# One encoder layer with 32 experts: rows split once into two-byte halves, expert 0's rows picked by one-hot matmuls, tables spread over expert 0's products

## The chip, the cores and the metric

The kernel runs on one core of one Trainium2 chip. The metric is the time of one execution on the device in microseconds (us), the median of three runs. The engines are called PE (TensorE), DVE (VectorE), ACT (ScalarE), POOL (GpSimd) and SP (SyncE, which here only issues transfers); PEld is PE's loading of stationary operands.

## The reference

One layer over 1024 tokens of width 1024, all in float32. What matters for the change is the end of the first half and the whole second half:

```python
h = layer_norm(ALPHA * h + mixed @ w_out, ln1_g, ln1_b)
logits = h @ w_router + b_router            # 32 experts
top_vals, top_idx = lax.top_k(logits, 4)
gates = softmax(top_vals)
# each expert e, for the tokens that chose it:
y = ((up + 1) * gate * sigmoid(1.702 * gate)) @ w_mlp2[e] + b_mlp2[e]
# gate = min(a, 7), up = clip(b, -7, 7), [a | b] = x @ w_mlp1[e] + b_mlp1[e]
h = layer_norm(ALPHA * h + sum over the 4 experts of gates * y, ln2_g, ln2_b)
```

Attention with a window, a multi-scale pool and two gated branches come before; the change leaves them as they are.

## The kernel before

Every float32 operand of a product is split into a two-byte high part (float16) and a two-byte low part (bfloat16), and each product is three matmuls: high by high, high by low, low by high. The instructions of each engine stand in the order in which the Python emits them (`manual_schedule`), so an engine that waits holds up all that is emitted for it later.

**The loop over the eight token tiles** (L587 to L617) ends the first half. For tile t it loads the old row, multiplies the mixed branches by `w_out` in two halves of 512 columns (`mth`, `mtl` hold the left operand as 8 slices by 1024 tokens), adds and normalises into the row `z`, and runs the router of earlier tiles in between: `hooks.transposed(t-1)` (eight float32 PE transposes of `z`, then `tr_out` splits them from PSUM: high half by ACT at L683, low half by DVE at L684), `logits(t-1)`, `topk(t-1)`, `pos_mm`, `place` and `gates(t-2)`, `tables(t-3)`. `hooks.step(t-1)` stands at the head of an iteration: ACT rounds one megabyte of expert 0's weights (L945) and DVE forms its low half (L950). `gates` (L742) takes the exponential of the four best logits on ACT, scales four one-hot rows by them and adds them up on DVE. `write` (L665) stores `z` twice, as `hD` (the rows that experts gather) and as `accD` (the sums).

**Behind the loop** `experts.main` (L978) takes the experts one after another, in an order `TURN` by their number of tokens; each has a fixed capacity (176 for the first, 109 to 188 for the others). An expert is six steps: four quarter products of the first matrix (L1090 to L1092), two halves of the second. The steps of neighbouring experts are interleaved in `seq`; expert 0's first four steps are steps 0 to 3, the next expert begins with step 4. Around step i the program emits: evacuation of step i-1, `post_v`, `post_a`, `post_p` (the gated activation), the split of the weights of step i+2 (`w_hi` on ACT, `w_lo` on DVE), then the matmuls. Four tables (`start`, `mid`, `end`, `x_evac`) hang further work on steps.

For an expert's rows: `onehot` builds a one-hot matrix of tokens by slots on DVE, `slot_mm` multiplies it with small columns (token number, gate) on PE, `gather` fetches the float32 rows by an indirect transfer that POOL issues (L1021), `x_tr` transposes them on PE in float32 (L1055), `x_hi` and `x_lo` split them (ACT L1066, DVE L1071).

Ahead of step 0 stand, for expert 0: slots, gather, transposes and split of its rows, and the first part of `ranks` (L773), which sorts the experts by their number of tokens, fetches expert numbers for the transfers and turns the biases. In the middle of step 0 `tables` runs the rest of `ranks`: gates' columns for all experts (L825 to L838), then the table of tokens beyond the capacities (L842 to L878); with expert 0's gates and the next expert's one-hots between. At the end of step 0 `first_rows` gathers the next expert's rows, which are transposed at the end of step 1.

Weights arrive in transfers of one megabyte that SP issues into nine buffers (`refill`); a buffer is free when DVE has formed its low half.

## Time and profile before

| | us |
|---|---|
| median of three runs (1866.14 to 1868.57) | 1866.81 |
| the profiled execution's own time | 1861.56 |
| its span, first to last instruction | 1859.7 |
| PE busy in the span | 1757.3 |
| DVE busy | 1528.2 |
| ACT busy | 1226.1 |
| POOL busy | 560.5 |

The span is one execution recorded by the hardware profiler. A line such as "L950 DVE ... wl<-raw,wh 128x2048" is line 950 of the kernel on VectorE, writing `wl` from `raw` and `wh`. Busy matmuls overlap one another, so a PE that is busy all the time is one that waits for nothing; what one matmul costs is read from the distance of two starts.

### The profile page before, as it was taken

The numbers are of one execution on the slowest core, as the hardware profiler recorded it, in microseconds if no ns is written. First come the engines' busy times: TensorE is split into PE (matmuls) and PEld (weight loads), VectorE is DVE, ScalarE is ACT, GpSimd is POOL, SyncE is SP. The second block draws the span as 40 slices with busy tenths as digits, with TensorE's granted clock in tenths as the row PEclk, the third lists the DMA queues.
The fourth block names the chain that finished last, engine by engine and source line by source line (L and its number), as shares of the span: only waits on it lengthen the run. The fifth ranks groups of instructions, "written<-read, shape, count | busy, mean of one in ns | idle before, by whom it ended". The sixth has DMA issues, their size and how long they took to land.

```text
span 1859.7 us, 53706 instructions
## 1 busy us (share of the span) xinstructions
PE 1757.3 (94%) x23150; PEld 1495.0 (80%) x23150; DVE 1528.2 (82%) x2184; ACT 1226.1 (66%) x1679; POOL 560.5 (30%) x586
## 2 busy tenths in 40 slices
PE   7998999999896899999999999999999999999990
PEld 6455554444444899999999999999999999999990
DVE  4587853234696989999989999999999999999985
ACT  4455532223121578888788788888888888888873
POOL 1336420000012532244323253233432542343211
PEclk9999999999997999999999999999999999999995
DMA  5100031112655699999999999999999999999975
GB/s 181 52 24 24 24 100 56 57 46 91 218 193 197 193 332 365 364 363 358 321 354 357 362 360 370 356 373 366 367 368 376 373 370 366 375 371 366 369 274 200
DMA packets 245955, 494.20 MB, mean 266 GB/s; under 512 B 10982, under 2 KB 32870, under 8 KB 245712
## 3 DMA queue, kind: packets, MB, share of 16 engines
q1 hardware_dynamic: 234432, 453.03, 67.5%
q0 software_dynamic: 10992, 36.62, 8.0%
q8 instruction: 184, 3.01, 0.7%
q10 hardware_dynamic: 288, 1.05, 0.1%
q14 instruction: 59, 0.48, 0.1%
HBM read 458.34 MB, written 32.33 MB: 264 GB/s over the span
## 4 chain that ended last, share of the span: by engine, by line
PE 80%; DVE 11%; ACT 3%; DMA 3%; issue 2%; POOL 0%; SPq 0%; POOLq 0%; DVEq 0%; ACTq 0%
PE mm L1090 19%; PE mm L1091 19%; PE mm L1092 19%; PE mm L110 4%; PE mm L109 4%; PE mm L111 4%; PE tr L1157 2%; PE tr L1055 2%; PE pb L109 2%; PE pb L111 2%; PE pb L110 2%; DMA raw<-in_w_mlp_dram 1%; DVE wl L950 1%; PE sl L1005 1%; DVE s L346 1%
## 5 line engine op out<-in xcount | busy, mean ns | idle before, releaser
L950 DVE SCALAR_TENSOR_TENSOR wl<-raw,wh 128x2048 bf16<-128x2048 f32 x384 | 874.5, 2286 | 46.4 <-ACT wh L945 46.1
L1090 PE MATMUL mm<-xh,wh 128*128 128x123 f16 (+30 forms) x4096 | 744.0, 223 | 0.6 <-ACT xh L1066 0.6
L1091 PE MATMUL mm<-xl,wh 128*128 128x123 bf16 (+30 forms) x4096 | 743.6, 223 | 0.3 <-DVE nv L747 0.3
L1092 PE MATMUL mm<-xh,wl 128*128 128x123 f16 (+30 forms) x4096 | 743.7, 223 | 0.0
L945 ACT ACTIVATE wh<-raw 128x2048 f16<-128x2048 f32 x384 | 725.5, 1909 | 12.6 <-PE mm L1091 8.8
L1091 PEld LDWEIGHTS <-wh 128*128 128x128 f16 x6144 | 598.2, 97 | 1.8 <-issue 1.0
L1092 PEld LDWEIGHTS <-wl 128*128 128x128 bf16 x6144 | 597.5, 97 | 2.5 <-issue 2.5
L1090 PEld LDWEIGHTS <-wh 128*128 128x128 f16 x6144 | 595.9, 97 | 0.9
L1091 PE MATMUL mm<-al,wh 128*128 128x123 bf16 (+30 forms) x2048 | 370.7, 222 | 1.9 <-DVE al L1148 1.9
L1090 PE MATMUL mm<-ah,wh 128*128 128x123 f16 (+30 forms) x2048 | 371.0, 223 | 0.3 <-ACT ah L1137 0.3
L1092 PE MATMUL mm<-ah,wl 128*128 128x123 f16 (+30 forms) x2048 | 370.8, 222 | 0.0
L1021 POOL DMA_INDIRECT x<-hD,ig x51 | 73.8, 1447 | 553.2 <-DVE st L1010 310.9
L1169 POOL DMA_INDIRECT accD<-y,is x51 | 120.3, 2359 | 225.6 <-ACT yT L1114 68.9
L109 PE MATMUL mm<-xth,wh 128*128 128x512 f16 x400 | 151.9, 380 | 1.2 <-DVE ypl L104 1.1
L110 PE MATMUL mm<-xtl,wh 128*128 128x512 bf16 x400 | 151.8, 380 | 0.0
L111 PE MATMUL mm<-xth,wl 128*128 128x512 f16 x400 | 151.7, 379 | 0.0
L1165 ACT ACTIVATE y<-tr,gt 128x512 f32<-128x512 f32 (+11 forms) x102 | 65.4, 679 | 91.7 <-PE tr L1157 48.7
L111 PEld LDWEIGHTS <-wl 128*128 128x128 bf16 x528 | 51.7, 98 | 62.5 <-issue 0.3
L110 PEld LDWEIGHTS <-wh 128*128 128x128 f16 x528 | 51.7, 98 | 56.8 <-issue 1.5
L109 PEld LDWEIGHTS <-wh 128*128 128x128 f16 x528 | 51.8, 98 | 55.2 <-issue 0.3
L163 DVE SCALAR_TENSOR_TENSOR wl<-raw,wh 128x768 bf16<-128x768 f32 (+1 forms) x30 | 24.3, 865 | 81.9 <-ACT wh L159 81.7
L1106 ACT ACTIVATE pre<-mm,b1r 128x176 f32<-128x176 f32 (+30 forms) x256 | 77.8, 370 | 12.7 <-PE mm L1092 12.5
(304 smaller groups left out, 2475.3 us busy)
## 6 DMA issues: line engine op xcount, KB each, us to landing
raw<-in_w_mlp_dram SPq DMA_DIRECT2D x384, 1024.0 KB, 11.9
raw<-in_w_in_dram SPq DMA_DIRECT2D x13, 1024.0 KB, 5.3
xt<-in_x_dram SPq DMA_DIRECT2D x16, 512.0 KB, 6.7
raw<-in_w_out_dram SPq DMA_DIRECT2D x4, 1024.0 KB, 5.1
a<-accD SPq DMA_DIRECT2D x8, 512.0 KB, 7.2
hD<-z SPq DMA_DIRECT2D x7, 512.0 KB, 2.7
accD<-z SPq DMA_DIRECT2D x7, 512.0 KB, 4.0
out_dram<-o SPq DMA_DIRECT2D x7, 512.0 KB, 2.7
```

The lines of the kernel that those rows point to most:

```text
L109: nc.tensor.matmul(ps, wh(k), xh(k), start=first and i == 0, stop=False)
L110: nc.tensor.matmul(ps, wh(k), xl(k), start=False, stop=False)
L111: nc.tensor.matmul(ps, wl(k), xh(k), start=False, stop=last and i == n - 1)
L945: nc.scalar.activation(WT[i][0][:, a:b], RAW[i, h], AF.Copy, scale=WS)
L950: nc.vector.scalar_tensor_tensor(lo[:, a:b], RAW[i, h], WS, hi[:, a:b], op0=OP.mult, op1=OP.subtract)
L1021: nc.gpsimd.indirect_dma_start(out=x[:n], out_offset=None, in_=hD, in_offset=IO(ap=ig[:n, c], axis=0))
L1090: nc.tensor.matmul(ps[:, j], wh[:, k, fs], h[:, k, :Cr], start=k == 0, stop=False)
L1091: nc.tensor.matmul(ps[:, j], wh[:, k, fs], l[:, k, :Cr], start=False, stop=False)
L1092: nc.tensor.matmul(ps[:, j], wl[:, k, fs], h[:, k, :Cr], start=False, stop=k == KT - 1)
L1106: nc.scalar.activation(o[:, j], ps[:, j], AF.Identity, scale=0.5 / WS, bias=b1r[:, f0 + g + j, r:r + 1])
L1165: nc.scalar.activation(E[r]["ys"][j][:n, c * 512:(c + 1) * 512], E[r]["yp"][j][:n].rearrange("p a b -> p (a b)"), AF.Copy, scale=E[r]["gt" ...
L1169: nc.gpsimd.indirect_dma_start(out=accD, out_offset=IO(ap=E[r]["is_"][:n, j:j + 1], axis=0), in_=E[r]["ys"][j][:n], in_offset=None, comput ...
```

## The change

- `mth` and `mtl` are laid out by token tile, and a tile's part of them is used again, once its products are done, for the row's high and low half: `row` writes the high half (ACT) and the low half (DVE) straight from `z`, for all 1024 columns at once, and the last normalisation steps also take 1024 columns at once, except for tile 7.
- `transposed` makes sixteen two-byte transposes of the halves and two copies, both on ACT. `hD` holds the two halves, 4096 bytes a row as before, stored by two transfers on SP's queue.
- `gates`: a second exponential on ACT over all 32 logits, one DVE instruction in place of three.
- Expert 0's rows are not gathered: 128 matmuls of the halves by its one-hots (`x0_mm`), most of them placed around tile 7's router, and eight evacuations (`x0_out`).
- The other experts' gathered halves are transposed in two-byte form and copied: one ACT and one DVE copy of up to 1024 columns.
- `ranks` yields once more; its parts stand in the middle and at the end of step 0, in the middle of step 1 and at the end of step 2. The next expert's rows are gathered in the middle of step 2 and transposed in the middle of step 3.
- The last steps take the activation ahead of the split of weights.

```diff
@@ loop over the token tiles
+        if t == NT - 1:
+            hooks.x0_mm(range(3), range(6))
+            hooks.pos_mm(t - 1)
+            hooks.x0_mm(range(3, 4), range(6))
+        if t < NT - 1:
+            ln.apply(z, g1, b1, z, slice(0, D))
+            hooks.row(t, 0, KT)
+        else:
+            for h in range(2):
+                ln.apply(z, g1, b1, z, slice(h * 512, (h + 1) * 512))
+                hooks.row(t, h * 4, h * 4 + 4)
+                hooks.x0_mm(range(4 + h, 5 + h), range(6))
         hooks.write(t, z)
     hooks.place(NT - 2)
-    for h in range(2):
-        hooks.tr_out(NT - 1, h)
+    hooks.transposed(NT - 1)
     hooks.logits(NT - 1)
     hooks.topk(NT - 1)
+    hooks.x0_mm(range(4), range(6, KT))
     hooks.pos_mm(NT - 1)
     hooks.place(NT - 1)
+    hooks.gates(NT - 2)
+    hooks.x0_mm(range(4, 7), range(6, KT))
+    hooks.x0_mm(range(6, 7), range(6))
+    hooks.x0_mm(range(7, 8), range(KT))
+    hooks.x0_out()
@@ Router
+    def row(self, t, a, b):
+        nc, (hi, lo) = self.nc, self.rows
+        z = self.z[t][:, a * P:b * P].rearrange("p (k q) -> p k q", q=P)
+        nc.scalar.activation(hi[:, t, a:b], z, AF.Copy)
+        nc.vector.tensor_sub(lo[:, t, a:b], z, hi[:, t, a:b])
+    def x0_mm(self, tiles, ks):
...
+            for k in (2 * k2, 2 * k2 + 1):
+                for t in tiles:
+                    for j in range(2):
+                        nc.tensor.matmul(self.px[k2][:, k % 2], self.rows[j][:, t, k], self.moe.oh0(t),
...
     def transposed(self, t):
-        for h in range(2):
-            self.tr_mm(t, h)
-            self.tr_out(t, h)
+        nc, tk = self.nc, slice(t * P, (t + 1) * P)
+        self.hT[t] = []
+        for j, (dt, ident) in enumerate(((F16, "ident16"), (BF16, "identb"))):
+            tp = self.pt.tile([P, KT, P], dt, name="tp")
+            for k in range(KT):
+                nc.tensor.transpose(tp[:, k], self.rows[j][:, t, k], self.C[ident])
+            o = self.hb.tile([P, KT, P], dt, name="hh" if j == 0 else "hl")
+            nc.scalar.activation(o, tp, AF.Copy)
+            self.hT[t].append(o)
+            row = self.rows[j][:, t]
+            nc.sync.dma_start(self.hD[tk, j * D:(j + 1) * D], (row.bitcast(F16) if j else row).rearrange("p k q -> p (k q)"))
@@ gates
         nc.scalar.activation(e4, vm[:, :4], AF.Exp, bias=nv, accum_out=den)
+        nc.scalar.activation(lg, lg, AF.Exp, bias=nv)
         nc.vector.reciprocal(den, den)
-        nc.vector.tensor_scalar(e4, e4, den, None, op0=OP.mult)
-        nc.vector.tensor_mul(eq, eq, e4[:, :, None].to_broadcast([P, 4, NE]))
-        nc.vector.tensor_reduce(G, eq.rearrange("p k e -> p e k"), axis=AX.X, op=OP.add)
+        nc.vector.scalar_tensor_tensor(G, lg, den, mask, op0=OP.mult, op1=OP.mult)
@@ experts: rows of one expert
         def xparts(r):
+            return [(i, s0, n, lo) for i, (s0, n) in enumerate(E[r]["tiles"]) for lo in range(2)]
         def x_tr(r, part):
+            i, s0, n, lo = part
+            dt, ident = ((F16, C["ident16"]), (BF16, C["identb"]))[lo]
+            tp = pt.tile([P, KT, n + n % 2], dt, name="tr")[:, :, :n]
+            for k in range(KT):
...
+        def x_out(r, part):
...
+            if lo:
+                nc.vector.tensor_copy(E[r]["xl"][:, :, s0:s0 + n], tp)
+            else:
+                nc.scalar.activation(E[r]["xh"][:, :, s0:s0 + n], tp, AF.Copy)
@@ experts: what hangs on the first steps
-        slot_mm(0, 0, 2)
-        gather(0)
...
-        at(mid, 0, tables)
-        at(end, 0, first_rows)
+        def order():
+            next(rk)
+            refill()
+            evac(0, *groups(0)[0])
+        def late():
+            next(rk)
+            LATE["y"] = [[LATE["a"].tile([P, D], F32, name=f"y{b}{j}") for j in range(2)] for b in range(2)]
+            for y in LATE["y"][0] + LATE["y"][1]:
+                nc.gpsimd.memset(y, 0.0)
+        def slots0():
+            slot_mm(0)
+            targets(0)
+            onehot(1)
+        at(mid, 0, next, rk)
+        at(end, 0, order)
+        at(mid, 1, next, rk)
+        at(end, 2, late)
+        at(end, 1, slots0)
+        at(mid, 2, slot_mm, 1)
+        at(mid, 2, gather, 1)
         for r in range(1, NR):
...
             for j, part in enumerate(parts):
...
+                if r == 1:
+                    at(mid, 3, x_tr, r, part)
+                    at(end, 3, x_out, r, part)
@@ experts: around a step
+            product = 0 < i <= NS and seq[i - 1][0] == 1
+            if product and i >= NS - 3:
+                post_a(i - 1)
+                post_p(i - 1)
+                product = False
             if split:
                 w_hi(n, 0)
```

## Rows read from the trace of the kernel before

**Rows 1.** The page: the chain that ended last, by engine.
```profile
PE 80%; DVE 11%; ACT 3%; DMA 3%; issue 2%; POOL 0%; SPq 0%; POOLq 0%; DVEq 0%; ACTq 0%
```

**Rows 2.** Busy time by stretch: us, PE, PEld, DVE, ACT, POOL, PE clock, DMA, GB/s.
```profile
480.00:570.00 90.00, 79.75 (x513) 40.08 (x513) 82.58 (x198) 18.43 (x33) 14.16 (x50) 0.98 0.50 176
572.65:573.26 0.61, 0.61 (x25) 0.59 (x24) 0.40 (x1) 0.00 (x0) 0.49 (x2) 1.00 0.04 13
600.00:615.00 15.00, 12.32 (x148) 11.72 (x147) 10.37 (x60) 2.63 (x4) 2.84 (x13) 0.85 0.07 22
615.00:640.00 25.00, 21.82 (x292) 21.37 (x290) 22.65 (x36) 14.48 (x17) 13.26 (x17) 1.00 0.72 220
1400.00:1500.00 100.00, 100.00 (x1646) 99.60 (x1644) 96.08 (x105) 85.53 (x102) 40.20 (x29) 1.00 1.05 371
```

**Rows 3.** DVE's timeline, one iteration of the token loop: start us, us, instruction.
```profile
540.36 2.29 DVE L950 SCALAR_TENSOR_TENSOR wl<-raw,wh 128x2048 bf16<-128x2048 f32 x1
...
544.41 0.14 DVE L747 TENSOR_SCALAR nv<-vm 128x1 f32<-128x1 f32 x1
...
546.08 1.28 DVE L684 TENSOR_TENSOR hl<-tp,hh 128x512 bf16<-128x512 f32 x2
547.28 0.68 DVE L604 SCALAR_TENSOR_TENSOR z<-pb,xt 128x512 f32<-128x512 f32 x1
...
549.04 0.18 DVE L708 SCALAR_TENSOR_TENSOR lg<-mm,br 128x32 f32<-128x32 f32 x1
...
551.11 0.74 DVE L76 SCALAR_TENSOR_TENSOR z<-z,ln_mv,g 128x512 f32<-128x512 f32 x1
...
554.01 2.29 DVE L950 SCALAR_TENSOR_TENSOR wl<-raw,wh 128x2048 bf16<-128x2048 f32 x1
```

**Rows 4.** ACT's timeline in the same iteration.
```profile
544.58 0.30 ACT L750 ACTIVATE e<-vm,nv 128x4 f32<-128x4 f32 x1 [8.21 <-DVE nv L747]
...
544.88 1.06 ACT L683 ACTIVATE hh<-tp 128x512 f16<-128x512 f32 x2
...
548.11 1.90 ACT L945 ACTIVATE wh<-raw 128x2048 f16<-128x2048 f32 x1
```

**Rows 5.** Timelines of DVE and ACT elsewhere: instructions of the new sizes.
```profile
1835.28 2.48 DVE L1508 SCALAR_TENSOR_TENSOR a<-a,sums,g 128x1024 f32<-128x1024 f32 x2
...
1828.52 1.06 ACT L1485 ACTIVATE j<-a 128x1024 f32<-128x1024 f32 x1 [11.76 <-DVE ln_st L59]
```

**Rows 6.** From tile 7 to step 4: a piece of the chain, then PE's timeline.
```profile
572.87 0.70 DVE z L604
...
595.96 0.31 PE L1090 MATMUL mm<-xh,wh 128*128 128x176 f16 x1 [0.58 <-ACT xh L1066]
...
639.95 0.22 PE L1090 MATMUL mm<-xh,wh 128*128 128x138 f16 x1
```

**Rows 7.** Busy time by stretch as in Rows 2, PE's clock behind the token loop.
```profile
576.00:578.00 2.00, 0.20 (x2) 0.10 (x1) 1.90 (x6) 0.00 (x0) 0.00 (x0) 0.77 1.05 406
...
598.00:600.00 2.00, 2.00 (x16) 2.00 (x14) 1.29 (x6) 0.39 (x2) 1.35 (x6) 0.50 1.04 384
```

**Rows 8.** Chain of waits: float32 transposes, of a short and of a full tile.
```profile
631.58 0.59 PE tr L1055 x8
...
665.99 0.44 PE tr L1055 x4
```

**Rows 9.** PE's timeline near the end: the wait before the last product.
```profile
1804.12 0.21 PE L1091 MATMUL mm<-al,wh 128*128 128x109 bf16 x1 [1.85 <-DVE al L1148]
```

**Rows 10.** The same DVE instruction beside POOL's memsets and without them.
```profile
625.73 2.64 DVE L1123 TENSOR_SCALAR pre<-pre 128x704 f32<-128x704 f32 x1
...
641.48 0.52 DVE L1123 TENSOR_SCALAR pre<-pre 128x704 f32<-128x704 f32 x1
```

**Rows 11.** Weights, issue to landing, for 640 to 840 us and 1640 to 1760 us.
```profile
DMA to landing us min/median/max: 5.5/8.1/10.3
...
DMA to landing us min/median/max: 13.8/15.6/19.4
```

More of the change, by code (lines that the diff above doesn't have):

```diff
@@ L665, in write @@
     def write(self, t, z):
-        nc = self.nc
-        q = nc.scalar if t == NT - 1 else nc.sync
-        q.dma_start(self.hD[t * P:(t + 1) * P, :], z)
+        q = self.nc.scalar if t == NT - 1 else self.nc.sync
         q.dma_start(self.accD[t * P:(t + 1) * P, :], z)
-    def tr_mm(self, t, h):
-        nc = self.nc
-        self.tp[t, h] = tp = self.pt.tile([P, 4, P], F32, name="tp")
-        for k in range(4):
-            nc.tensor.transpose(tp[:, k], self.z[t][:, (h * 4 + k) * P:(h * 4 + k + 1) * P], self.C["identf"])
@@ new lines, in x0_mm @@
+    def x0_mm(self, tiles, ks):
+        nc, c = self.nc, self.moe.c0
+        for k2 in range(ks[0] // 2, (ks[-1] + 2) // 2):
+            if k2 not in self.px:
+                ps = self.pb.tile([P, 512], F32, name="pb") if k2 < 3 else self.pt.tile([P, 4, P], F32, name="tp")
+                self.px[k2] = (ps if k2 < 3 else ps.rearrange("p a b -> p (a b)"))[:, :2 * c].rearrange("p (k c) -> p k c", c=c)
+            for k in (2 * k2, 2 * k2 + 1):
+                for t in tiles:
+                    for j in range(2):
+                        nc.tensor.matmul(self.px[k2][:, k % 2], self.rows[j][:, t, k], self.moe.oh0(t),
+                                         start=t == 0 and j == 0 and k % 2 == 0, stop=t == NT - 1 and j == 1 and k % 2 == 1,
+                                         skip_group_check=True)
@@ L1019, in gather, with targets @@
                 nc.vector.tensor_copy(ig[q, c], E[r]["pl"][q, i, 0:1])
-                x = wk1.tile([P, D], F32, name=f"x{i}")
+                x = wk1.tile([P, 2 * D], F16, name=f"x{i}")
                 nc.gpsimd.indirect_dma_start(out=x[:n], out_offset=None, in_=hD, in_offset=IO(ap=ig[:n, c], axis=0))
                 xs.append(x)
-            rows(r, 0, 5 if r else 2)
+            E[r].update(xs=xs, xh=None)
+            targets(r)
+        def targets(r):
+            E[r]["st"] = st = sm.tile([P, 2, 8], F32, name="st")
+            E[r]["is_"] = is_ = sm.tile([P, 2], I32, name="is")
+            for i, (s0, n) in enumerate(E[r]["rows"]):
+                nc.vector.tensor_copy(st[:n, i, :5], E[r]["pl"][:n, i, :5])
             for i, (s0, n) in enumerate(E[r]["rows"]):
@@ L1215, in main @@
             if r > 1:
[L1216 to L1218 removed]
+                at(start, max(b - 9, 3), onehot, r)
+                at(end, max(b - 8, 3), slot_mm, r)
+                at(start, max(b - 7, 4), gather, r)
             parts = xparts(r)
             for j, part in enumerate(parts):
[L1221 to L1224 removed]
+                if r == 1:
+                    at(mid, 3, x_tr, r, part)
+                    at(end, 3, x_out, r, part)
+                else:
+                    s_ = b - 1 - len(parts) + j
+                    at(end, s_, x_tr, r, part)
+                    at(x_evac, s_ + 1, x_out, r, part)
         def run(table, i):
@@ L1248, in main @@
                 w_hi(n, 1)
-            if 0 < i <= NS and seq[i - 1][0] == 1:
+            if product:
                 post_p(i - 1)
@@ L1257, in main @@
                         run(mid, i)
-                    if j < len(gs) - 1:
+                    if i and j < len(gs) - 1:
                         evac(i, g, nf)
```

161 lines of the change are left out of this document (66 added, 95 removed).

## The prediction

> **What bounds the kernel now.** I first read the page's chain by engine: PE carries four fifths of it [rows 1]. Busy time by stretch says where that holds and where it does not [rows 2]. Inside the experts (1400 to 1500 us) PE is busy 100.00 of 100.00 us, with DVE at 96.08 close behind and DMA moving 371 GB/s; an instruction of another engine is worth nothing there, a PE instruction is worth its own length. In the token loop (480 to 570) it is the other way round: DVE is busy 82.58 of 90 us and PE 79.75. Between loop and experts (600 to 640) neither is full. So the change is priced in three places: the loop by DVE's order, the passage by its chain, the rest by PE.
>
> In DVE's timeline of one iteration [rows 3] one instruction follows another; from one weight split at 540.36 to the next at 554.01 an iteration takes 13.65 us. ACT is mostly idle there and runs ahead: its rounding of the next weights starts at 548.11, six us before DVE asks for them [rows 4].
>
> **The loop.** I lay the new order on the same iteration, counting from the weight split as 0, for tiles 2 to 5.
> - The gates start at 4.05 (544.41) and last 1.67 us, up to 546.08. One DVE instruction replaces three, but it waits for a second exponential on ACT, which I take at the 0.30 us of the first [rows 4]: 1.05 us in all, so 0.6 less.
> - The two subtractions from PSUM go: 546.08 to 547.28, 1.20 us less. The second half of `z` is then added at 5.1 and the logits are wanted 1.76 us later (547.28 to 549.04), at 6.86.
> - They come later than that. ACT, held by the exponentials until 4.8, now makes two copies of 1024 columns, 1.06 us each by the row of that width [rows 5], up to 6.9; then come the 24 small matmuls of the logits (25 PE instructions in 0.61 us at 572.65, the logits' [rows 2]). DVE waits 0.7 us, for 7.5.
> - Top-4 and the refinement of the root take 2.07 us (549.04 to 551.11): 9.6. Normalising took four instructions, 2.90 us (551.11 to 554.01); two of 1024 columns take 2.40 by the row with two such [rows 5]: 12.0, 0.5 less.
> - Now the low half, on DVE, needs the high half from ACT: 1.06 us in which DVE has nothing else in its order; the subtraction itself takes about 1.2 (half of the 2.48 that the two of 1024 columns take in rows 5). ACT's rounding of the next weights now stands behind the high half instead of ahead of it: 12.0 + 1.06 + 1.90 and the hand-overs give 15.1 for the next split.
>
> That is 15.1 against 13.65, 1.4 us more for each of four tiles. Tile 0 has no gates, no old subtraction and no wait: 3.05 more at its end, 0.5 less in normalising, 2.55. Tile 1 loses 1.2 of that again, 1.35. Tile 6 has no weights behind it, 0.7. Tile 7's first half is shorter by 1.8. In sum tile 7's second half starts 8.5 us later than at 572.87. PE needs about 12 us an iteration and gives no help. Ends: 5 if ACT's hand-overs cost less than I put, 10.4 if tile 7 gives nothing back. POOL's copies keep their place; on SP two 256 KB stores take the place of one, with no one waiting.
>
> **From tile 7 to step 4.** Before, this takes 67.1 us: 572.87 to 639.95 [rows 6], of which expert 0's matmuls start at 23.1. In the new order, from the start of tile 7's second half: its sums, the root and tile 6's top-4 up to 3.9 (3.83 in rows 3); normalising, high and low half for 512 columns at a time up to 9.3; transposes and two ACT copies up to 11.3, logits 12.0 (1.9 us later than before); top-4 and place 14.2. PE has 40 of the 128 one-hot matmuls left at 13.5, when tile 7's positions are issued. Between 615 and 640 us 292 matmuls, nearly all of 176 columns, took 21.82 us [rows 2], 0.0747 each; 40 take 3.0, up to 16.5. So expert 0 starts at about 16.7 instead of 23.1: gather, float32 transposes and their split are gone.
>
> From there PE has at most 12.32 + 21.82 = 34.1 us of work up to step 4 [rows 2], and could be there at 51; DVE cannot. Between 600 and 640 us DVE was busy 10.37 + 22.65 = 33.0 us [rows 2]: six weight splits, columns, overflow table, one-hots, activations. All of it stays ahead of step 4's rows, now behind step 0 (96 matmuls, 7.2 us) and the ranks' first matmuls and biases (3.2 us, an estimate: 40 matmuls more and a hand-over): 16.7 + 7.2 + 3.2 + 33.0 = 60.1, and 61 with the last copy of the next expert's rows. The stall for their gather falls under this, so it costs nothing unless DVE gets shorter; then the gather is late next.
>
> The clock adds to that. Behind the loop PE's granted clock fell from 1.00 to 0.50 (1.2 of 2.4 GHz) while it had next to nothing to do, at 576 to 578, and was still 0.50 at 598 to 600, in matmuls; from 615 on it was 1.00 [rows 2, 7]. The one-hot matmuls fill the first part of the hole and leave about 6 us of it. Ends: 0 if the clock holds, 5 if it stays low through step 0; I take 2.5. Sum 63.5: 3.6 us less than before. Ends: 7 less, and 0.
>
> **The experts.** A full tile's eight float32 transposes take 0.88 us (four in 0.44), a short tile's 0.59 [rows 8]. Sixteen two-byte ones: of 128 columns, at 0.0747 × 128 / 176 = 0.054 us, take 0.87 (an estimate); for a short tile, at the 0.61 / 24 = 0.0254 us of the small logits matmuls [rows 2], 0.41. So the full tiles stay the same and eighteen experts with a short second tile save 0.18 each: 3.3 us on a PE that is full. Ends: 0 and 4. ACT's copies keep their length, DVE's get shorter by 0.2 to 0.8 us an expert, both beside PE, worth nothing while PE is full.
>
> **The end.** The last product's low half now stands ahead of a weight split on DVE, and PE's wait of 1.85 us for it goes [rows 9]. But ACT's rounding is then behind the activation, so the last split ends some 2 us later and PE waits about 1 us for that. I take 0.8 less. Ends: 2 and 0.
>
> **Sum:** +8.5 - 3.6 - 3.3 - 0.8 = +0.8 us on the profiled execution's own 1861.56, so 1862.4. That execution lies 5.25 us below the median of 1866.81; on the median I forecast 1867.6, no difference within 0.2% (3.7 us), about what a measurement of this kernel can tell from no change. The loop's loss and the passage's gain both lie on the path, and nearly cancel with the experts' gain.
>
> **Rivals.**
> 1. *Slower: the passage gains nothing.* The place is steps 0 to 3. If the clock stays at 0.50 until step 0 has ended, 5 instead of 2.5, and DVE is held up by POOL, the passage takes 68: +8.5 + 0.9 - 4.1 = +5.3, 1872. It decides from 66.5 us of passage on. For it: `late` puts POOL's four memsets at the end of step 2, ahead of the next one-hots on DVE, and one DVE instruction took 2.64 us beside those memsets where it took 0.52 without them [rows 10]. Against it: in 40 us DVE lost only that much. The Trainium skill (SBUF — State Buffer, Who interferes with whom) has DVE's two-port modes and GpSimd lock one another out for a whole instruction; the trace agrees with 2.64 against 0.52 us. By that rule alone the forecast would rise by up to 2.1 us.
> 2. *Faster: the loop loses nothing.* If ACT's high half and the rounding behind it cost DVE no wait (the hand-overs are fewer, or PE and not DVE sets the iteration), +8.5 becomes 0 to +1 and the sum is -7, 1860. For it: DVE's own work gets shorter by about a us per tile. Against it: DVE's order, in which the low half stands directly behind the high half.
> 3. *The experts give nothing back.* Weights took 8.1 us to land early and 15.6 late [rows 11], so the transfers fall behind while PE is full. If the transfers have become the bound by the end, PE's 3.3 us are lost in a wait for weights: +4.1, 1871.
>
> **How the numbers follow.** Forecast 0.36, rival 1 0.23, rival 2 0.31, rival 3 0.10. Faster by over 0.2% is rival 2: 0.31. Within: 0.36. Slower: rivals 1 and 3, 0.33. The forecast's own range is 1864 to 1871. The range for 8 in 10 takes in rivals 2 and 1 with their own unknowns (the loop at 5 and the passage 7 less: 1858.9; the loop at 10.4 and the passage at 0: 1873.1, with 2.1 from POOL 1875.2): 1859 to 1875.
>
> **What would show it.** Right: weight splits 15 us apart in the loop, a DVE wait for ACT's high half of 1 us in each; tile 7's second half at about 581; expert 0's first matmul about 17 us behind it; DVE full from there to step 4, with PE waiting 4 us or so for the last copy; PE's clock at 0.50 for some us around the start of step 0; short tiles' sixteen transposes in 0.4 us. Wrong: iterations of 13.7 us or less, PE idle within the experts, or ACT waiting for weights at the end.

## The result and the profile after

The changed kernel takes 1879.25 us (median of 5 runs, 1875.78 to 1880.85) where the kernel before takes 1866.14 (1863.22 to 1868.57): the ratio is 1.0069, with a 95% interval of 1.0053 to 1.0084. The forecast was 1867.6, no difference, with a range of 1859 to 1875. The profiled execution of the changed kernel is the median one, with a span of 1877.5 us; that of before, with a span of 1859.7, was a quick one, so the two traces differ by 17.8 us and the medians by 13.1. A second profile of each kernel (below) lies 16.4 apart.

The traces are compared in four stretches: up to tile 7's second half of `z` (the loop), from there to step 4 (the passage), from step 4 to the end of PE's last transposes (the experts), and the rest (the end). In us, with all other kernels of this study, which the experiments below explain:

| kernel | loop | passage | experts | end | span | ratio to before (95%) |
|---|---|---|---|---|---|---|
| before | 572.87 | 67.08 | 1176.08 | 43.67 | 1859.7 | |
| changed | 583.40 | 69.91 | 1177.59 | 46.60 | 1877.5 | 1.0069 (1.0053 to 1.0084) |
| forecast, against before | +8.5 | -3.6 | -4.1 | 0 | +0.8 | |
| before, second profile | 572.25 | 65.96 | 1176.64 | 43.55 | 1858.4 | |
| changed, second profile | 584.96 | 67.63 | 1177.29 | 44.92 | 1874.8 | 1.0076 (1.0062 to 1.0090) |
| loop in another order | 575.69 | 69.60 | 1177.38 | 45.73 | 1868.4 | 1.0034 (1.0021 to 1.0047) |
| fourth transpose later | 584.54 | 62.34 | 1181.31 | 45.61 | 1873.8 | 1.0073 (1.0060 to 1.0086) |
| leftover table later | 583.78 | 61.01 | 1179.82 | 45.29 | 1869.9 | 1.0062 (1.0048 to 1.0076) |
| tables earlier | 585.03 | 67.81 | 1177.38 | 46.08 | 1876.3 | 1.0071 (1.0056 to 1.0086) |
| y transposes behind | 585.04 | 67.82 | 1178.40 | 45.84 | 1877.1 | one execution |
| before with two parts | 569.57 | 68.30 | 1179.34 | 43.09 | 1860.3 | 0.9983 (0.9972 to 0.9993) |
| four edits | 575.41 | 59.24 | 1181.23 | 45.92 | 1861.8 | 0.9993 (0.9984 to 1.0003) |
| table in pieces | 575.46 | 59.07 | 1177.63 | 45.64 | 1857.8 | 0.9978 (0.9968 to 0.9988) |
| ... and 16 memsets | 574.50 | 58.87 | 1177.50 | 46.53 | 1857.4 | 0.9977 (0.9966 to 0.9989) |
| ... and 30 matmuls | 572.44 | 58.55 | 1177.87 | 45.34 | 1854.2 | 0.9972 (0.9960 to 0.9985) |

So the changed kernel lost 10.5 us in the loop, 2.8 in the passage, 1.5 in the experts and 2.9 at the end. All four (the forecast's -0.8 for the last product lies in the experts' stretch) came out worse than forecast, by 2.0, 6.4, 5.6 and 2.9. The second pair of profiles has the same signs and other sizes: 12.7, 1.7, 0.7 and 1.4.

**The loop.** DVE's timeline of one iteration of the changed kernel, which answers to [rows 3]; the bracket is the idle time before the instruction and who ended it:

```profile
549.51 2.29 DVE L978 SCALAR_TENSOR_TENSOR wl<-raw,wh 128x2048 bf16<-128x2048 f32 x1 [0.57 <-ACT wh L973]
...
562.77 1.22 DVE L687 TENSOR_TENSOR mtl<-z,mth 128x1024 bf16<-128x1024 f32 x1 [1.12 <-ACT mth L686]
564.58 2.29 DVE L978 SCALAR_TENSOR_TENSOR wl<-raw,wh 128x2048 bf16<-128x2048 f32 x1 [0.58 <-ACT wh L973]
```

An iteration takes 15.07 us (549.51 to 564.58) instead of 13.65. DVE now stands still twice at its end, 1.12 us for the row's high half and 0.58 for the next weights' rounding, which ACT used to have ready six us ahead. ACT's timeline of the same iteration, which answers to [rows 4], shows the two in one chain behind DVE's own normalising:

```profile
561.68 1.06 ACT L686 ACTIVATE mth<-z 128x1024 f16<-128x1024 f32 x1 [4.38 <-DVE z L77]
562.65 1.90 ACT L973 ACTIVATE wh<-raw 128x2048 f16<-128x2048 f32 x1
```

**The passage.** Expert 0's first matmul starts 20.45 us behind tile 7's second half (583.40 to 603.85) instead of 23.09. But step 4 starts at 653.31, 69.91 behind it, later than before. PE's timeline from the transposes of expert 1's rows to step 4:

```profile
636.53 0.62 PE L1099 MATMUL tr<-ident,x 128*128 128x128 f16 x8 [1.89 <-DMA x<-hD,ig]
...
639.32 0.37 PE L1099 MATMUL tr<-ident,x 10*128 10x10 f16 x8 [1.72 <-DMA x<-hD,ig]
646.34 0.35 PE L1099 MATMUL tr<-identb,x 10*128 10x10 bf16 x8 [6.64 <-ACT xh L1110]
...
653.31 0.23 PE L1129 MATMUL mm<-xh,wh 128*128 128x138 f16 x1
```

Four groups of transposes stand ahead of step 3's second half, each in a PSUM tile of its own, and the pool has three such tiles (`e_pt`, L1034). The fourth waits 6.64 us for ACT to copy the first one out, and everything behind it on PE waits too. Busy time by stretch (columns as in [rows 2]) shows who is full meanwhile:

```profile
604.00:614.00 10.00, 9.79 (x174) 9.50 (x172) 3.29 (x16) 2.40 (x4) 1.71 (x7) 1.00 0.01 3
614.00:634.00 20.00, 19.65 (x277) 19.44 (x278) 19.21 (x44) 10.81 (x13) 8.33 (x12) 1.00 0.94 342
634.00:640.00 6.00, 2.09 (x33) 1.64 (x31) 5.67 (x20) 0.00 (x0) 5.19 (x14) 0.85 0.78 257
640.00:646.00 6.00, 0.00 (x0) 0.00 (x0) 5.79 (x19) 3.81 (x5) 0.00 (x0) 0.50 0.11 19
646.00:652.00 6.00, 5.66 (x47) 5.64 (x46) 3.39 (x6) 0.42 (x2) 0.95 (x1) 0.52 0.87 271
```

From 614 to 646 DVE is busy 30.67 of 32 us, while PE is busy 2.09 us of the 6 up to 640, in which its granted clock falls, and not at all from 640 to 646; the matmuls behind that run at 0.50 (1.2 of 2.4 GHz). ACT is late because an instruction ahead of its copy waits for DVE, and DVE was in the table of leftover tokens, 633.57 to 641.64. ACT's timeline:

```profile
642.19 0.79 ACT L1171 ACTIVATE th<-pre 128x704 f32<-128x704 f32 x1 [9.31 <-DVE pre L1148]
...
645.27 1.15 ACT L1110 ACTIVATE xh<-tr 128x1024 f16<-128x1024 f16 x2
```

**The experts.** Between 1420 and 1520 us PE is busy for the whole time, as before. What its transposes take is read from start to start. First the kernel before, y transposes, x transposes and the matmuls behind them, and then one short tile; then the changed kernel, the same kinds, and at its end y transposes ahead of a tile of 110 rows:

```profile
664.95 1.04 PE L1157 MATMUL tr<-identf,yT 128*128 128x128 f32 x8
665.83 0.60 PE L1055 MATMUL tr<-identf,x 128*128 128x128 f32 x4
666.26 0.22 PE L1090 MATMUL mm<-xh,wh 128*128 128x138 f16 x1
...
672.12 0.66 PE L1055 MATMUL tr<-identf,x 8*128 8x8 f32 x8
672.71 0.45 PE L1005 MATMUL sl<-cols,oh 128*128 128x5 f16 x9
```

```profile
672.57 0.61 PE L1099 MATMUL tr<-identb,x 128*128 128x128 bf16 x8
673.01 0.22 PE L1129 MATMUL mm<-xh,wh 128*128 128x138 f16 x1
...
678.77 1.04 PE L1196 MATMUL tr<-identf,yT 128*128 128x128 f32 x8
679.75 0.35 PE L1099 MATMUL tr<-ident,x 8*128 8x8 f16 x8
680.03 0.23 PE L1129 MATMUL mm<-xh,wh 128*128 128x138 f16 x1
...
911.80 1.03 PE L1196 MATMUL tr<-identf,yT 128*128 128x128 f32 x8
912.67 0.55 PE L1099 MATMUL tr<-ident,x 110*128 110x110 f16 x8
```

A short tile took 0.59 us in float32 (672.12 to 672.71) and takes 2 x 0.28 in two halves (679.75 to 680.03): next to nothing is saved. A full tile took 2 x 0.43 and takes 2 x 0.44. And the y transposes, which the change does not touch, take 0.97 or 0.98 instead of 0.88 wherever the two-byte transposes of a short tile (2 to 60 rows) follow them directly, 17 times of 17. Where those of a tile of 109 to 128 rows follow, they take what they took before, 13 times of 13 (0.87 from 911.80 to 912.67). PE's weight loads show what a short group is made of; before, then after:

```profile
672.11 0.57 PEld L1055 LDWEIGHTS tr<-identf,x 8*128 8x128 f32 x8
```

```profile
679.74 0.26 PEld L1099 LDWEIGHTS <-x 8*128 8x128 f16 x8 [0.20 <-issue]
```

A single two-byte load has a row of 0.10 us, so eight in 0.26 start 0.16 / 7 = 0.023 us apart, and eight transposes 0.023 apart are 0.18 of the 0.28. The other 0.10 I read as an edge, the price of going from the short group to the next kind of work. In float32, with 0.14 for a single load, it is 0.43 / 7 = 0.061 apart, 0.49 of the 0.59, and one edge of 0.10. Two short halves have two edges. The 0.10 that the y transposes gain is a third, on the near side of the short group; a full tile's 0.44 is 8 x 0.055 and shows none. In the kernel before no short tile stands directly behind y transposes, so whether a short float32 group would cost the same there is not shown. Over all of step 4 to the last product, x and y transposes together take 79.9 us before and 81.8 after: x 35.7 and 35.95, y 44.2 and 45.9.

**The end.** PE's wait of 1.85 us [rows 9], and one of 0.32 ahead of it, are gone; three short ones of 0.56, 0.44 and 0.37 stand in their place, and up to PE's last transposes the end is 0.6 us shorter. Behind them ACT's last copy and POOL's last scatter, before and then after:

```profile
1816.07 0.69 ACT L1165 ACTIVATE y<-tr,gt 109x512 f32<-109x512 f32 x1 [0.45 <-PE tr L1157]
...
1817.52 1.52 POOL L1169 DMA_INDIRECT accD<-y,is  x1 [5.98 <-ACTq L1287]
```

```profile
1830.94 0.69 ACT L1204 ACTIVATE y<-tr,gt 109x512 f32<-109x512 f32 x1 [0.45 <-PE tr L1196]
...
1833.56 1.53 POOL L1208 DMA_INDIRECT accD<-y,is  x1 [7.89 <-issue]
```

From the end of the copy to the scatter it is 0.76 us before and 1.93 after. Within the latter wait the DMA view shows two packets of the instruction queues (`q8`, `q14`), within the former none. From the scatter to the end of the span it took 1.7 us longer in this execution.

### The profile page after: what moved, and what is told of

Same layout as the page of the kernel before. It is cut to its first block, busy times and chain, and to the rows that moved or that the text cites. A ratio compares the mean times of both kernels' runs of the same rounds, so it can differ in the third digit from the quotient of the medians.

```text
span 1877.5 us, 54612 instructions
## 1 busy us (share of the span) xinstructions
PE 1764.8 (94%) x23644; PEld 1501.0 (80%) x23702; DVE 1506.1 (80%) x2114; ACT 1240.5 (66%) x1666; POOL 510.8 (27%) x584
## 3 DMA queue, kind: packets, MB, share of 16 engines
q8 instruction: 188, 3.08, 0.7%
## 5 line engine op out<-in xcount | busy, mean ns | idle before, releaser
L1208 POOL DMA_INDIRECT accD<-y,is x51 | 92.0, 1804 | 246.7 <-DMA accD<-y,is 80.5
L110 PE MATMUL mm<-xtl,wh 128*128 128x512 bf16 x363 | 137.6, 379 | 0.0
```

The costliest lines, as they stand in the source:

```text
L110: nc.tensor.matmul(ps, wh(k), xl(k), start=False, stop=False)
L1208: nc.gpsimd.indirect_dma_start(out=accD, out_offset=IO(ap=E[r]["is_"][:n, j:j + 1], axis=0), in_=E[r]["ys"][j][:n], in_offset=None, comput ...
```

## The experiments

**Both kernels once more.** What was expected of the kernel before:

> The kernel before once more, unchanged, for a second profile: which stretch differs between two executions of one kernel. If the 2.9 us by which the changed kernel's end (from PE's last transpose to the end of the span) is longer than before's 43.7 us is the change's, this run shows 43.7 again; if it is the spread of executions, it shows 44 to 47. Time 1862 to 1869.

And of the changed one:

> The changed kernel once more, unchanged: a second profile of it and its times beside the kernels of this call. If the stalls that the first profile shows are the kernel's and not one execution's, this one has the 6.6 us wait of PE for ACT's copy in step 3 again, 69 to 70 us from tile 7's second half to step 4, and an end of 45 to 47 us behind PE's last transposes; 0.6 to 0.8% slower than before.

Before gave 1860.21 us, below the 1862 to 1869 expected, and an end of 43.55; changed gave 1877.62, an end of 44.92, and PE's wait for ACT's copy again, 5.5 us this time because the gather's two tiles came 1.6 and 1.2 us later (their transposes start at 638.13 and 640.55). Its passage took 67.63 us where 69 to 70 were expected. The end of 43.1 to 43.7 in three profiles of before and its variant, and of 44.9 to 46.6 in all eleven of the changed kernel and its variants, is therefore the change's. The constant part of it is the 1.17 us ahead of the scatter: 0.76 in each of the three, 1.92 or 1.93 in each of the eleven. From the scatter to the end of the span it is 41.6 to 42.2 us against 42.2 to 43.9, two ranges that touch.

**The loop's order.** ACT's rounding of the next weights ahead of the row's high half, DVE's weight split ahead of the row's low half:

```diff
-        hooks.step(t - 1)
...
+        self.moe.prefetch_hi(w)
         nc.scalar.activation(hi[:, t, a:b], z, AF.Copy)
+        self.moe.prefetch_lo(w)
         nc.vector.tensor_sub(lo[:, t, a:b], z, hi[:, t, a:b])
```

> Token loop only: the rounding of the next weights stands ahead of the row's high half on ACT, and the weights' low half ahead of the row's low half on DVE, so that both roundings run beside work of DVE. Theory (the loop's loss is the two waits of DVE for ACT, 1.12 and 0.57 us in each iteration of 15.06): iterations of about 13.4 us, tile 7's second half at about 573 to 575 instead of 583.4, and some 9 to 10 us less at the end than the changed kernel's 1879, 1869 to 1870. Rival (the loop is longer because PE or SP's stores set the iteration): iterations stay above 14.5 us, less than 3 us gained, 1876 or more.

1869.1 us, 8.5 less than the changed kernel's 1877.62 (by the ratios 6.5 to 7.8, with intervals that do not meet), and tile 7's second half at 575.69. DVE's timeline shows both waits gone and an iteration of 13.18 us:

```profile
516.19 2.28 DVE L979 SCALAR_TENSOR_TENSOR wl<-raw,wh 128x2048 bf16<-128x2048 f32 x1
...
529.37 2.28 DVE L979 SCALAR_TENSOR_TENSOR wl<-raw,wh 128x2048 bf16<-128x2048 f32 x1
```

What DVE waited for in the loop (total, times, longest), changed kernel and then this one:

```profile
DVE mtl L687 <- ACT mth L686: 6.9, 6, 1.2
DVE wl L978 <- ACT wh L973: 3.5, 6, 0.6
```

```profile
DVE z L604 <- PE pb L111: 5.4, 5, 3.6
...
DVE mtl L688 <- ACT mth L686: 1.1, 1, 1.1
```

The theory holds: 10.4 us of waiting for ACT became 1.1, and the iterations are shorter than before's 13.65. What is left against before, 2.8 us, is above all one new wait of 3.6 us in tile 1. The row's low half now stands behind 2.3 us of weight split, PE meets its transpose in the middle of tile 1's second product and runs the nine matmuls behind it 0.43 us apart, at a granted clock of 0.50, and DVE waits for them. Tiles 2 to 6 win 2.4 us against before; tile 7, and the stretch up to tile 0's second half, lose 1.9 together.

**The fourth transpose.** It is put behind the second half of step 3's matmuls and behind the first three copies out of PSUM:

```diff
-                    at(mid, 3, x_tr, r, part)
-                    at(end, 3, x_out, r, part)
+                    if j < 3:
+                        at(mid, 3, x_tr, r, part)
+                    else:
+                        at(end, 3, x_tr, r, part)
+                    if j == len(parts) - 1:
+                        table = end[3]
+                        last = [table.pop()] if j == 3 else []
+                        for q, pp in enumerate(parts):
+                            if q == 3:
+                                table += last
+                            table.append((x_out, (r, pp)))
```

> Only the order in step 3: the fourth transpose of expert 1's rows stands behind the second half of step 3's matmuls and behind the first copy out of PSUM, instead of ahead of both. Theory (PE's 6.65 us wait for ACT's copy is a wait for the fourth of three PSUM buffers, and the clock's fall behind it follows from it): the second half of step 3 starts at about 640 instead of 646.6, step 4 at about 649.5 to 651 instead of 653.3, 2.5 to 4 us less, 1875 to 1877. Rival (DVE, late by its own work, sets step 4's start in any order): PE waits as long ahead of step 4, the clock falls there, and less than 1.5 us is gained, 1878 or more.

1875.77 us: inconclusive in time, and telling in the trace. Step 4 starts 62.34 us behind tile 7's second half instead of 67.6 to 69.9, more than expected. But the experts take 1181.31 instead of 1177.3 to 1177.6: PE waits for DVE's copy right behind step 4's first matmul, and the granted clock falls once more behind that wait (0.66 in the mean of 649 to 652).

```profile
649.14 0.22 PE L1130 MATMUL mm<-xl,wh 128*128 128x138 bf16 x1 [2.03 <-DVE xl L1108]
```

From tile 7's second half to PE's last transposes it is 1243.65 us, against 1247.50 and 1244.92 in the changed kernel's two profiles, and the ratio of 1.0073 lies between the changed kernel's 1.0069 and 1.0076. So the PSUM tile is where PE waits; what it waits for is DVE. With the tile out of the way the work of DVE holds step 4 up instead, as the rival said.

**The table of leftover tokens.** Moved from the end of step 2 to the end of step 5, with its memsets:

```diff
-        at(end, 2, late)
+        at(end, 5, late)
```

> Only the table of tokens beyond the capacities and the four memsets on POOL behind it, moved from the end of step 2 to the end of step 5, where PE is full. Theory (step 3 waits for DVE, which spends 8.1 us from 633.57 to 641.64 on that table, 2.8 of it because one instruction takes 3.08 us beside the memsets): step 4 about 7 to 8 us earlier, at 645 to 646, with PE's wait of 6.65 us gone or under 1 us and no second fall of its clock; 1871 to 1873. Rival (the gather, which landed for the second tile at 639.3, or ACT's copy is next and just as late): less than 3 us gained, 1876 or more. A third: DVE is as full in the experts, so that the table's 8 us come back as waits of PE behind step 5, nothing gained.

1873.82 us, 3.8 less than the changed kernel's 1877.62 (by the ratios 1.3 to 2.6, with intervals that overlap, so in time no gain is shown; from tile 7's second half to PE's last transposes the trace has 1240.83 against 1247.50 and 1244.92). The passage takes 61.01 us, 6.6 to 8.9 less, and PE's wait in step 3 is gone:

```profile
PE tr L1099 <- DMA x<-hD,ig: 2.7, 2, 2.1
```

In the trace that is the theory. Of the gain 2.2 to 2.5 us are lost again in the experts, as the third case said in part: at 673.50 PE waits 1.14 us for DVE's copy of the next rows, again with the table ahead of it.

**The tables earlier.** Half a step for each part behind the second one, the gather included:

```diff
-        at(mid, 1, next, rk)
-        at(end, 1, slots0)
-        at(mid, 2, slot_mm, 1)
-        at(mid, 2, gather, 1)
+        at(end, 0, next, rk)
+        at(mid, 1, slots0)
+        at(end, 1, slot_mm, 1)
+        at(end, 1, gather, 1)
```

> The tables of ranks half a step earlier: the third part directly behind the second at the end of step 0, expert 0's slots and the next one-hots in the middle of step 1, the next expert's slots and gather at the end of step 1. Theory (DVE is what step 4 waits for, and it stood nearly idle from 604 to 613 because the parts of ranks are queued on PE behind 48 matmuls each): DVE gets full 3 to 4 us earlier and step 4 starts 3 to 4 us earlier, about 66.5 instead of 69.9 behind tile 7's second half; some 3 us less than the changed kernel. Rival (closer together, each part has PE wait for DVE or ACT and back): PE gets new waits of 2 us and more in steps 0 and 1, gather lands no earlier against PE's place, and less than 1 us is gained.

Nothing gained (67.81 us of passage, ratio 1.0071), and not for the rival's reason either: PE has no new waits in steps 0 and 1, and the gather lands in time.

```profile
604.00:614.00 10.00, 9.86 (x174) 9.66 (x173) 3.14 (x17) 0.60 (x3) 1.70 (x7) 1.00 0.02 6
614.00:634.00 20.00, 19.45 (x269) 18.82 (x266) 19.20 (x44) 12.72 (x14) 10.38 (x15) 1.00 0.92 327
```

```profile
646.49 0.35 PE L1099 MATMUL tr<-identb,x 10*128 10x10 bf16 x8 [9.64 <-ACT xh L1110]
```

DVE is mostly idle up to 614 and full from 614 on, 3.14 and 19.20 us against 3.29 and 19.21: its full stretch begins behind the second part, which turns the biases and which I had not moved, and the sum of its work is the same. PE, two gather waits the earlier, waits 9.64 us instead of 6.64 for the same copy. That the gather's 3.6 us went and step 4 stayed shows again that it is DVE's work that sets it.

**The y transposes behind the x transposes**, in each step:

```diff
+            run(end, i)
             if 0 < i <= NS and seq[i - 1][0] == 2:
                 y_tr(i - 1)
-            run(end, i)
```

> In each step the float32 transposes of a product's result stand behind the two-byte transposes of the next rows instead of ahead of them; nothing else. Theory (a two-byte transpose directly behind a float32 one costs PE 0.1 us, as the y transposes' 0.97 to 0.98 us where x transposes follow and 0.87 to 0.88 where matmuls follow say): every such group takes 0.88 us, and PE needs 1.6 us less from step 4 to its last transposes, 1176.0 instead of 1177.6. Rival (the 0.1 us is the price of any change between float32 and two-byte transposes): the sum of y and x transposes stays, 1177.6. Time 1877 to 1879 either way; this is read from the trace.

The theory as it stands falls: already in the changed kernel the 0.10 is there only beside short tiles. The rival holds for the most part: the y transposes behind a short tile take 0.93 us in this order, between 0.88 and 0.98, those behind a long one 0.89, and all of them together 45.18 us, against 45.89 in the changed kernel and 44.23 before. Of 1.66 us 0.7 are to be had by the order, too little to see in the total.

**The kernel before with two parts of the change**, the shorter gates and normalising 1024 columns at a time:

```diff
-        nc.vector.tensor_scalar(e4, e4, den, None, op0=OP.mult)
-        nc.vector.tensor_mul(eq, eq, e4[:, :, None].to_broadcast([P, 4, NE]))
-        nc.vector.tensor_reduce(G, eq.rearrange("p k e -> p e k"), axis=AX.X, op=OP.add)
+        nc.scalar.activation(lg, lg, AF.Exp, bias=nv)
+        nc.vector.scalar_tensor_tensor(G, lg, den, mask, op0=OP.mult, op1=OP.mult)
...
+        if t < NT - 1:
+            ln.apply(z, g1, b1, z, slice(0, D))
```

> The kernel before with two parts of the change alone, both in the token loop: the shorter gates (one product of the exponentials, the reciprocal of their sum and the mask in place of three instructions) and normalising 1024 columns at a time for tiles 0 to 6. Rows, transposes and the gather of expert 0 stay as before. Theory (the loop is bound by DVE's order, and it is the row split, not these two parts, that made it longer): iterations of 12.5 to 12.9 us instead of 13.65, tile 7's second half 5 to 7 us earlier than at 572.9, 0.25 to 0.4% faster than before. Rival (PE, some 12 us an iteration, or the late transposes behind a whole row set the iteration): iterations of 13.3 us and more, under 0.1% gained.

1860.51 us against 1863.18, ratio 0.9983: faster, by less than expected. The iteration is as expected, 12.88 us from one weight split to the next (512.43 to 525.31). Tile 7's second half is at 569.57, 2.7 to 3.3 us earlier than in the two profiles of before rather than 5 to 7. In its profiled execution the passage took 1.2 to 2.3 us longer than before's, and PE's two waits ahead of the last product 1.63 and 2.18 us, where before had 0.32 and 1.85 (0.86 and 1.85 in its second profile), which gave much of it back; whether these belong to the edit was not tried. Against the changed kernel's 583.40 to 584.96 it shows the price of the row split in the loop: 14 to 15 us, of which the loop's other order takes 8 to 9 off.

**Four edits together**: the loop's order, the tables earlier, the leftover table at the end of step 4, the y transposes behind. The first, second and fourth are the diffs above; the third is

```diff
-        at(end, 2, late)
+        at(end, 4, late)
```

> Four edits together: the loop's order of the first experiment, the tables half a step earlier, the table of leftover tokens with its memsets at the end of step 4, and the y transposes behind the x transposes. Theory (each removes a loss of its own): tile 7's second half at 575 to 576, step 4 some 57 to 59 us behind it, PE's part behind that 1176 to 1177, 45.5 us of end: 1854 to 1858 of span, 0.1 to 0.4% faster than the kernel before. Rival (they remove the same wait, and the next one, PE's own matmuls or the gather, stands right behind it): passage 61 us or more, 1860 or more, no faster than before.

1862.85 against 1863.57, ratio 0.9993: no faster. Loop and passage are about as the theory had them (575.41 and 59.24), the span is the rival's (1861.8); the experts take 1181.23, with PE waiting 1.3 us for DVE's activation in step 6 and 1.0 for DVE's copy of the next rows.

**The table in pieces**: the same without the last edit, the leftover table cut into four pieces of DVE work at the ends of steps 14, 18, 22 and 26 (by three more `yield` in `ranks`, with a space of their own for its small tiles, not shown), and POOL's memsets at the end of step 4:

```diff
-        at(end, 2, late)
+        at(end, 4, ymem)
+        at(end, 14, next, rk)
+        at(end, 18, next, rk)
+        at(end, 22, next, rk)
+        at(end, 26, next, rk)
```

> The changed kernel with the loop's order of the first experiment, the tables half a step earlier, and the table of leftover tokens cut in four pieces at the ends of steps 14, 18, 22 and 26, with the memsets on POOL at the end of step 4. Theory (the table's 8 us of DVE in one piece cost PE a wait wherever DVE is as full as it is up to step 8; in pieces of 2 us they fit into DVE's gaps): no wait of PE over 0.5 us from step 4 to the last product, 1177 to 1178 us there, step 4 at 57 to 59.5 us behind tile 7's second half; 1857 to 1859 of span, 0.1 to 0.4% faster than before. Rival (it is the bunched expert 0 work itself that fills DVE): PE waits 1 us and more in steps 4 to 8 again, no faster than before.

1858.47 against 1863.18, ratio 0.9978: this version is faster than both kernels. Against the kernel before with only two parts of the change, 0.9983, it is not: the intervals overlap. All waits of PE from step 4 to the end:

```profile
PE tr L1208 <- ACT yT L1165: 1.1, 1, 1.1
PE mm L1141 <- ACT ah L1188: 0.6, 1, 0.6
PE mm L1142 <- DVE al L1199: 0.4, 1, 0.4
PE mm L1143 <- DVEq L1360: 0.4, 1, 0.4
```

All four stand at the last products; up to there PE waits for nothing, and the experts are back at 1177.63. The table with its 8 us on DVE cost 7 to 9 us in the passage, 2 to 4 behind step 4 or 5, and nothing in pieces where DVE has gaps. Not all of that is the pieces: wherever table and memsets stood together, one DVE instruction of the table took 2.9 to 3.1 us instead of 0.2, and here, with the memsets apart from it, none of DVE's instructions beside them is longer than usual. The two parts of the edit were not tried one by one.

**16 more instructions on POOL**, added to the version before this:

```diff
+        padt = kb.tile([P, 2], F32, name="padt")
+        for _ in range(16):
+            nc.gpsimd.memset(padt, 0.0)
```

> The kernel with the spread table, and 16 memsets of 128x2 on POOL ahead of the experts, which do no work. Theory (the last scatter starts 1.93 us behind ACT's last copy in every profile of the changed kernel and 0.76 in every profile of before, and only in the former does a packet of the instruction queue fall into that wait: POOL waits for its next instructions; 16 instructions more move that fetch to an earlier place, where POOL is idle): 0.76 us again, the end 44.5 instead of 45.6 us behind PE's last transposes, 1.2 us less of 1858.5. Rival (the fetch is another engine's, or the wait is the scatter's own): 1.93 us stays.

1859.31 us, ratio 0.9977, and the wait is 1.93 us still, with the packets of the instruction queues in it. The theory in this form falls. That the instruction queues are at work in the wait is seen in every one of these profiles; which engine's instructions they carry, and why before has none there, stays open.

**30 matmuls into the hole behind the loop**, on the version with the table in pieces:

```diff
     hooks.place(NT - 2)
+    hooks.fill(30)
     hooks.transposed(NT - 1)
```

> The kernel with the spread table, and 30 matmuls of 160 columns into a part of PSUM that nothing reads, ahead of tile 7's transposes, where PE is idle for 2.3 us behind the token loop. Theory (the clock's fall to 0.50 behind the loop comes of that idle time and costs expert 0 some 2 us): the granted clock stays at 1.00 or falls for under 3 us, expert 0's first matmul 18 us behind tile 7's second half instead of 20.1, step 4 1 to 2 us earlier. Rival (the shorter holes around the logits are enough for the fall, or DVE sets step 4's start whatever PE does): less than 0.5 us.

Busy time by stretch behind the loop, without them and with them (this kernel's loop ends 3 us earlier in its profile):

```profile
584.00:586.00 2.00, 1.27 (x13) 0.84 (x14) 1.17 (x4) 1.45 (x3) 0.21 (x1) 0.77 0.72 285
586.00:588.00 2.00, 1.30 (x28) 1.19 (x29) 0.26 (x2) 0.84 (x1) 0.00 (x0) 0.50 1.07 282
588.00:590.00 2.00, 2.00 (x17) 2.00 (x16) 1.23 (x6) 0.00 (x0) 0.00 (x0) 0.50 1.00 266
590.00:592.00 2.00, 2.00 (x19) 2.00 (x16) 1.02 (x6) 0.60 (x3) 0.20 (x1) 0.52 1.03 372
```

```profile
584.00:586.00 2.00, 2.00 (x36) 2.00 (x33) 1.21 (x7) 0.00 (x0) 0.00 (x0) 0.69 1.01 251
586.00:588.00 2.00, 2.00 (x18) 2.00 (x17) 1.04 (x6) 0.59 (x3) 0.00 (x0) 0.50 0.95 357
588.00:590.00 2.00, 2.00 (x28) 2.00 (x26) 0.25 (x1) 0.37 (x2) 1.21 (x5) 0.95 1.05 406
```

The time at 0.50 shrinks to about half, but expert 0 starts 19.57 us behind tile 7's second half instead of 20.09, and step 4 at 58.55 instead of 59.07: 0.5 us, the rival's figure. 1858.66 us, ratio 0.9972, not to be told from 0.9978.

## Why the prediction was wrong

**The loop: right in kind and nearly in size.** The period was forecast at 15.1 and is 15.07, for the reason given, and the loop's order shows it by experiment. The term was 8.5 and measured 10.5. Tile 0 is as forecast (2.49 us against 2.55), and so are tiles 2 to 5 (5.7 against 5.6). Tile 1 lost 2.36 instead of 1.35, in a stretch where PE's granted clock had fallen to 0.50 (489 to 494 us), which the sum left out of the loop. And tiles 6 and 7 together gave nothing back (18.82 us from tile 6's split to tile 7's second half, 18.86 before) where I had counted 1.1: tile 7 has no weight split ahead of it, and DVE waits 1.46 us for PE. Only the period repeats: the second pair of profiles has 5.8 for tiles 2 to 5 again, but 3.8 for tile 0, 1.5 for tile 1 and 1.6 for tiles 6 and 7.

**The passage: the step that failed.** The forecast was 63.5 us; it took 69.9. Of its parts:
- Tile 7's positions came at 14.4 instead of 13.5, the 40 matmuls behind them, at a clock of 0.50 up to 600.6, took 4.5 us instead of 3.0, and the copies of expert 0's rows 1.5 where I had 0.2. Expert 0 started at 20.45 instead of 16.7; I had the clock in the sum as 2.5, but behind DVE's work and not ahead of it. In the second profile, with the clock at 1.00 again from 599 on, it started at 18.95.
- DVE got full at 29.8 us, not 27.1. All of that is expert 0's late start: from there it was 9.4 us, where I had 7.2 + 3.2. That DVE sets step 4 was right. Its last copy for step 4 ended 66.0 us behind tile 7's second half (649.40), where the forecast had 61.
- Of these 5 us 2.7 are that late start. Another 2.8 are one instruction, 3.08 us beside POOL's memsets, with POOL's row and DVE's last copy behind it:

```profile
636.62 3.08 DVE L892 TENSOR_SCALAR y<-y,ecol 128x32 f32<-128x32 f32 x1
636.94 2.72 POOL L1242 MEMSET y<- 128x1024 f32 x3
...
648.61 0.79 DVE L1108 COPY xl<-tr 128x1024 bf16<-128x1024 bf16 x2
```

Its twin in the line before took 0.24. Where the memsets met other instructions of the table it was another one that took so long (in the runs with the tables earlier and with the leftover table later, a copy of two columns, 2.95 or 2.96 us instead of 0.17). This was rival 1's mechanism, put at up to 2.1 us and left out of the sum. By the rule of the Trainium skill (SBUF — State Buffer, Who interferes with whom) a DVE instruction in a two-port mode and one of GpSimd lock each other out of a shared port pair for the whole instruction. The trace agrees: DVE's instruction ended at 639.70, behind the third of three memsets (639.66).
- The last 3.9 us, from DVE's copy at 649.40 to step 4 at 653.31, I did not see at all: four groups of transposes for three PSUM tiles, PE held at the fourth, and then 48 matmuls in 6.1 us, most of them at a clock of 0.50 (3.6 at the 0.0747 us of the prediction). I had counted the engines' work and not the buffers between them. As the second experiment shows, this is where the loss stood but not what it was worth: without it DVE's lateness shows in step 4 itself.

So the gain of 3.6 was a loss of 2.8 (1.7 in the second pair of profiles), on the way of rival 1 with a second mechanism. Of rival 1's two conditions POOL's held; the clock was back at 1.00 before step 0 began and fell again in step 3.

**The experts: a term left out.** A short tile's sixteen two-byte transposes were put at 0.41 us, 16 x 0.0254, from the 24 logits matmuls [rows 2]. They do follow one another at 0.023 us. But float32's 0.59 [rows 8] held 0.10 of edge, and I set it against a price without any: two groups have two edges, and 2 x (0.18 + 0.10) is 0.56. The 3.3 us of gain fell to 0.4 for the seventeen short tiles behind step 4, full tiles lost 0.6, and 1.66 us were lost on the y transposes directly ahead of the short ones, 0.10 each. With that a short tile in two halves costs more than it did in float32. I took the price of one instruction from the middle of a long run of its kind for groups of eight.

**The end.** PE's part was forecast at -0.8 and is -0.6. Behind it the forecast was zero, and 1.4 to 2.9 us were lost: 1.17 ahead of the last scatter, in all profiles and for a cause that stays open, and the rest in the scatter and behind it, which varies.

**The range.** Its lower end does not follow from its terms: a loop of +5, a passage of -7 and -4.1 for the rest give 1860.7 on the median, not 1858.9. The measured time lies beyond the upper end, 1875.2, which had the loop at 10.4, the passage at no gain and 2.1 for POOL, and still the experts' gain in full.

Rival 3 (transfers become the bound) did not happen: no wait of PE in the experts is for a weight.

## What to carry to other kernels

When a change spares one engine work by having another split it in two, look at who waits for whom within one iteration: moving the next weights' two instructions ahead of the new ones gave back some 8 of 10.5 us here. Work that no one needs for a long time (a table for later, a memset) cost about its full length in a stretch that its engine bounded and nothing where that engine had gaps: place it by the engine's busy share, in pieces, and not beside what holds it up. Try the small parts of a change on the old kernel alone: two of them gave 0.9983 there, and the whole change with all its repairs 0.9972 to 0.9978, with intervals that overlap, so that nothing here shows a gain from the split rows themselves. And price a short group of instructions with its edges and its neighbours, from a whole group in the trace and not from one instruction inside a long run.

## What the runs showed of the hardware

- A group of eight two-byte transposes took 0.28 or 0.29 us for anything from 2 to 28 rows, 0.10 us more than eight times the 0.023 at which its weight loads follow one another; in float32 0.59 or 0.60. For 128 rows it took 0.44, 8 x 0.055.
- Eight float32 transposes took 0.97 or 0.98 us instead of 0.88 with the two-byte transposes of a short tile (2 to 60 rows) directly behind them, 0.93 with them directly ahead, and 0.87 or 0.88 with those of a tile of 109 or 110 rows behind.
- A DVE instruction that met POOL's memsets of 128x1024 ended only behind the last of three that followed one another: 3.08 us instead of 0.24, 2.95 instead of 0.17.
- In all eleven profiles of the changed kernel and its variants the wait between the last copy and the last scatter was 1.92 to 1.93 us, with packets of the instruction queues in it, and 0.76 without them in the three of the kernel before.
- PE's granted clock fell to 0.50 behind the loop and again in step 3, each time after PE had stood nearly idle (2.3 us up to 592.3; 2.09 us busy of the 6 from 634 to 640). In the version with the table in pieces, halving the time at 0.50 ahead of expert 0 was worth 0.5 us.
